# A two-layer hybrid decoder trunk: the first SwiGLU takes the stages of the inner ones, and the first norm's factors change place

## The chip, the core and the metric

The kernel runs on one core of a Trainium2 chip. The metric is device time in microseconds (us) of one execution, the median of the runs shown; lower is better. In the text the engines are TensorE (PE in the profile, its weight loads PEld), VectorE (DVE), ScalarE (ACT), GpSimd (POOL) and SyncE (SP). Each runs its own queue of instructions in order and waits on semaphores for the others. DMAs are issued from the queues of SP, ACT and POOL. L12 is line 12 of the kernel.

## What is computed

512 tokens of width 1024, two layers, each with a SwiGLU, a mixer (attention and short convolution) and a second SwiGLU, all float32 at the edges. The part that matters here:

```python
D_MODEL, SEQ, DEPTH, D_FF = 1024, 512, 2, 2816

def rms_norm(x, gain):
    inv = lax.rsqrt(jnp.mean(x * x, axis=-1, keepdims=True) + NORM_EPS)
    return x * inv * gain

def swiglu(h, w_gate, w_up, w_down):
    return (jax.nn.silu(h @ w_gate) * (h @ w_up)) @ w_down

for l in range(DEPTH):
    x = x + 0.5 * swiglu(rms_norm(x, ffn1_norm[l]), ffn1_wg[l], ffn1_wu[l], ffn1_wd[l])
    h = rms_norm(x, mix_norm[l])
    z = h @ w_in[l]                     # q, k, v and three convolution streams
    x = x + concat([attention(z), short_conv(z)]) @ w_out[l]
    x = x + 0.5 * swiglu(rms_norm(x, ffn2_norm[l]), ffn2_wg[l], ffn2_wu[l], ffn2_wd[l])
return rms_norm(x, final_norm)
```

## The kernel before

**Layout.** x is kept transposed, channels on partitions: eight tiles xs[c] of 128 channels x 512 tokens. At the start the token rows of x are loaded (xin), turned by TensorE (turn_x) and copied into xs (copy_x).

**Products in two parts.** Each float32 operand is split into a high part in a rounded format (a cast on ScalarE) and the rest (a subtraction on VectorE): `split`, L228. A product is three matmuls: high by high, high by low, low by high. Weight tiles are 128 x 1024 elements (512 KB), loaded into the tag "raw" (8 buffers) and split into "wh" and "wl" (3 buffers each). `take_split` hands out the next one and asks for the split two further on and for loads further ahead. A split marked "far" (`split_far`, L230) leaves VectorE out: ScalarE writes the high part and the negative, and a DMA on POOL's queue adds the raw tile to it.

**Blocks, pairs and shared down products.** The inner width 2816 is 11 blocks of 256. A "p" stage (`plain`) computes one block with the tile multiplied straight: four groups of 24 matmuls of 512 columns, two for the gate and two for up, then the split of the product. It uses the tile before the norm's factor, and multiplies by the factor `norm.inv` afterwards. A "w" stage (`winograd2`) computes two blocks with seven products in place of eight: weights of both are combined (s1, s2, s3, s4: sums by DMA in POOL's queue and by VectorE, L267 and L299), and the normed tile is combined into seven forms b11, b21, t2, t3, t1, t4, b22 of 1024 elements, each with a split of its own (`Seven.make`; the sums for t2, t3, t1 and t4 are additions on VectorE). It goes in seven steps in the order of CHAINS, two weight tiles each, 12 matmuls of 512 columns a tile, with tokens standing in the array (`stream`, L832). For this a norm first needs its factors, then eight scaled tiles hf (`Norm.scale`, L561). A "u" stage (`winograd`, L1013) is the same for one block, with 256 columns a matmul. A "d" stage is a straight down product of one block or two, whose eight results are added to xs (L1327). An "s" stage (`share`) is a down product of four blocks by seven products: either weights standing and 256 columns a matmul (`stand`, L817), added to xs directly, or tokens standing and 512 columns (`stream`), collected apart in rows of tokens (`Apart`) and turned back, by DMA in three quarters and by eight TensorE transposes in the last.

**Stages.** The first SwiGLU of layer 0 runs the list FIRST: two plain blocks, four pairs, a single block 10 by "u", and down products with weights standing. Layer 0's second SwiGLU and layer 1's first run INNER: one plain block, five pairs, shared down products with tokens standing, and a last straight down product of two blocks. The last SwiGLU has a list of its own.

**Order.** Most instructions are ordered by a planner at build time, in the program's order where they are ready. The opening (from `with tc.manual_schedule`, L721) is ordered by hand on TensorE, ScalarE and VectorE: spin, turn x, split the first three weight tiles in halves (`own`), form the split tile (`take`), squares of x for the norm (`squares`, four sets), and the products of groups 0 to 2 (`go`). The factors of the first norm (`first_parts`, two diagonal matrices, then two matmuls "ssq" and a copy into inv on ScalarE) are made behind it, within group 3. A warm-up at the start loads ScalarE's table for Silu. The mask for attention (`make_bias`, twelve small VectorE operations) is made behind the second down product.

Of the kernel before, what the change touches and what calls it, by code (L numbers as in the profile page):

```python
# [16 lines left out]
P = 128  # L17
D = 1024
# [59 lines left out]
def trunk_kernel(  # L78
# [157 lines left out]
    def need_split(g):  # L236
        while state["split"] <= min(g, len(order) - 1):
# [31 lines left out]
            else:  # L269

                need_raw(u + 4 + LOAD_AHEAD)
                a11, a12, s1, s3, a22 = (raw_of.get(u + i) for i in range(5))
                if what == "s2":
                    nc.vector.tensor_add(a11, a11, s1)
                if what == "s4":
                    nc.vector.tensor_add(a11, a11, a12)
                raw = {"a11": a11, "a12": a12, "s2": a11, "s3": s3, "s1": s1, "a22": a22, "s4": a11}[what]
                if what == FORMS[-1]:
                    for i in range(5):
                        del raw_of[u + i]  # L280
# [91 lines left out]
    def plan():  # L372
# [10 lines left out]
        def up(wg, wu, b):  # L383
            top, low = ((w, k, KC // 2, 2 * b * P, 2 * P) for w, k in ((wu, 0), (wu, KC // 2)))
            first = (wg, 0, KC // 2, 2 * b * P, 2 * P)
            u = add_unit(first)
            add_unit((wg, KC // 2, KC // 2, 2 * b * P, 2 * P))
            add_unit(top, low)
            add_unit(top, first)
            add_unit(low)  # L390
            order.extend((u, what) for what in FORMS)

# [9 lines left out]
        def ffn(wg, wu, wd, stages):  # L402
            for what, b in stages:
                how = "far" if b == (0,) and stages is not FIRST else None
                if what == "p":
                    plain(wg, wu, b)
                if what == "u":
                    up(wg, wu, b)
# [26 lines left out]
        for l in range(DEPTH):  # L435
            ffn(ffn1_wg[l], ffn1_wu[l], ffn1_wd[l], INNER if l else FIRST)
# [26 lines left out]
    class Norm:  # L463
        def __init__(self, i):
            self.i = i
            self.h = [None] * KC
            self.acc = None
            self.inv = None
            self.pairs = {}
            self.begun = set()  # L470
            self.order = range(KC)
# [85 lines left out]
        def scale(self, room):  # L557

            full = [g8(f"hf_{self.i}_{n}", F32, (P, KC // 2, S)) for n in range(2)]
            for c in range(KC):  # L560
                nc.vector.scalar_tensor_tensor(  # L561
                    full[c // 4][:, c % 4, :],
                    xs[c],
                    gain_of(self.i, c),
                    self.inv,
                    op0=ALU.mult,
                    op1=ALU.mult,
                )
            self.seven = Seven(full, room, f"{self.i}")
            self.make, self.forms = self.seven.make, self.seven.forms  # L570

    class Seven:
# [8 lines left out]
        def make(self, *names):  # L581
            for what in names:
                if what in self.forms:
# [3 lines left out]
                    full[j][:, :, t * H : (t + 1) * H] for j in range(2) for t in range(2)  # L587
# [39 lines left out]
    def room_stock(name):  # L627
        return [stock(f"sum{n}_{name}", shape=(P, KC // 2, H)) for n in range(2)]

# [30 lines left out]
    nc.scalar.activation(warm, warm, AF.Silu)  # L660
# [59 lines left out]

    with tc.manual_schedule(engines={pe, act, dve}):  # L721
# [19 lines left out]
        squares(0)  # L741
# [1057 lines left out]
```

## Time and profile before

| | us |
|---|---|
| median of 3 runs | 1640.02 |
| lowest and highest run | 1639.68, 1640.02 |
| profiled execution: span from first to last instruction | 1637.9 |
| TensorE busy in it | 1627.8 (99%) |
| VectorE busy | 1378.1 (84%) |
| ScalarE busy | 1141.7 (70%) |
| HBM read | 262.71 MB |

Of the profiled execution the span alone is listed; what lies before its first and behind its last instruction is not in it. In a row of the timeline the first number is the start in us from the span's start, the second the length, then engine, line, operation, output and inputs by their names in the program, shape, count, and in brackets how long the engine stood idle before and what ended that. "x2" after a shape means that two instructions of a kind follow each other without a pause. Matmuls are pipelined, and the length shown for one (390 ns for 512 columns) is longer than the step to the next.

### The profile page before, as it was taken

The page shows a single profiled execution, that of the slowest core. Times are in us where ns is not written, and L with a number is a line of the kernel's source. Part 1 is how long each engine was busy: PE and PEld are TensorE (multiplying, and loading weights), DVE is VectorE, ACT ScalarE, POOL GpSimd, SP SyncE. Part 2 cuts the span into 40 slices and gives each one's busy share as a digit, 9 for nine tenths or more (in the row PEclk, how much of TensorE's full clock was granted, in tenths as well). Part 3 has the DMA queues.
Part 4 walks back from the last instruction along what each step waited for, and adds up shares of the span by engine and source line. Part 5 has one row for each costly group of instructions (what it writes and reads, how often), then busy time and mean ns, then how long its engine had stood idle before and what let it go on. Part 6 is the DMA issues. An engine that isn't in the chain of part 4 may idle for free.

```text
span 1637.9 us, 21943 instructions
## 1 busy us (share of the span) xinstructions
PE 1627.8 (99%) x8012; PEld 1373.7 (84%) x8012; DVE 1378.1 (84%) x1812; ACT 1141.7 (70%) x1479; POOL 213.1 (13%) x188
## 2 busy tenths in 40 slices
PE   9999999999999999999999999999999999999998
PEld 7888889988898888888888888888888988888886
DVE  7987779987899977798998777989788998777997
ACT  6447786467767577777865777788586766777665
POOL 0011111100121011111011111110012111111121
PEclk9999999999999999999999999999999999999999
DMA  8378997742597698999866999998135967999992
GB/s 258 84 199 213 220 251 181 172 135 65 130 231 177 179 223 206 218 220 237 232 144 173 226 215 226 207 239 219 52 91 153 233 142 190 226 219 224 237 258 74
DMA packets 293984, 310.30 MB, mean 189 GB/s; under 512 B 110508, under 2 KB 179188, under 8 KB 293876
## 3 DMA queue, kind: packets, MB, share of 16 engines
q1 hardware_dynamic: 253284, 226.44, 48.1%
q0 software_dynamic: 39872, 81.80, 29.2%
q8 instruction: 63, 1.03, 0.3%
q10 hardware_dynamic: 720, 0.66, 0.1%
q14 instruction: 45, 0.37, 0.1%
HBM read 262.71 MB, written 2.10 MB: 162 GB/s over the span
## 4 chain that ended last, share of the span: by engine, by line
PE 90%; DVE 5%; ACT 3%; DMA 1%; issue 1%; SPq 0%; ACTq 0%; DVEq 0%
PE x L832 25%; PE y L832 13%; PE acc L326 7%; PE acc L327 7%; PE acc L329 7%; PE w L832 6%; PE x_s L832 5%; PE x_m L817 3%; PE y_s L832 3%; PE x_s L817 2%; PE w_s L832 2%; PE y_s L817 1%; PE y_m L817 1%; DVE wl L228 1%; PE acc L712 1%; PE x_e L832 1%
## 5 line engine op out<-in xcount | busy, mean ns | idle before, releaser
L228 ACT CAST wh<-raw 128x1024 fp32r<-128x1024 f32 (+1 forms) x491 | 511.1, 1045 | 346.0 <-PE x L832 91.4
L228 DVE TENSOR_TENSOR wl<-raw,wh 128x1024 fp32r<-128x1024 f32 (+1 forms) x491 | 598.1, 1226 | 175.7 <-ACT wh L228 174.3
L327 PE MATMUL acc<-xl,wh 128*128 128x512 f32 x424 | 165.9, 391 | 0.2 <-DVE xl L482 0.2
L326 PE MATMUL acc<-xh,wh 128*128 128x512 f32 x424 | 165.6, 392 | 0.0
L329 PE MATMUL acc<-xh,wl 128*128 128x512 f32 x416 | 162.3, 390 | 0.0
L223 POOL DMA_DIRECT2D raw<-in_ffn_wu_dram x39 | 48.8, 1252 | 392.9 <-DMA raw<-in_ffn_wu_dram 233.7
L327 PEld LDWEIGHTS acc<-xl,wh 128*128 128x128 f32 x424 | 79.7, 188 | 16.5 <-DVE xl L482 0.6
L326 PEld LDWEIGHTS acc<-xh,wh 128*128 128x128 f32 x424 | 79.8, 188 | 15.9
L329 PEld LDWEIGHTS acc<-xh,wl 128*128 128x128 f32 x416 | 78.2, 188 | 16.3
L223 POOL DMA_DIRECT2D raw<-in_ffn_wg_dram x39 | 48.2, 1259 | 231.5 <-DMA raw<-in_ffn_wu_dram 115.4
L223 POOL DMA_DIRECT2D raw<-in_ffn_wd_dram x34 | 41.0, 1209 | 244.6 <-DMA raw<-in_ffn_wd_dram 95.8
L267 DVE TENSOR_TENSOR raw<-raw,raw 128x1024 f32<-128x1024 f32 x56 | 68.1, 1222 | 2.3 <-DMA raw<-in_ffn_wu_dram 1.8
L1163 ACT COPY raw_a<-turned 128x1024 uint16<-128x1024 uint16 x48 | 63.1, 1356 | 0.0
L832 PE MATMUL w<-wh,fb21h 128*128 128x512 f32 x152 | 59.2, 390 | 0.0
L832 PE MATMUL x<-wh,ft2h 128*128 128x512 f32 x152 | 59.2, 390 | 0.0
L832 PE MATMUL y<-wh,ft3h 128*128 128x512 f32 x152 | 59.2, 390 | 0.0
L832 PE MATMUL x<-wh,ft1l 128*128 128x512 f32 x152 | 59.1, 389 | 0.0
L832 PE MATMUL x<-wl,ft1h 128*128 128x512 f32 x152 | 59.1, 389 | 0.0
L832 PE MATMUL w<-wl,fb21h 128*128 128x512 f32 x152 | 59.1, 389 | 0.0
L832 PE MATMUL x<-wl,ft2h 128*128 128x512 f32 x152 | 59.1, 389 | 0.0
L832 PE MATMUL w<-wh,fb21l 128*128 128x512 f32 x152 | 59.1, 389 | 0.0
L832 PE MATMUL x<-wh,ft2l 128*128 128x512 f32 x152 | 59.1, 389 | 0.0
(611 smaller groups left out, 4649.2 us busy)
## 6 DMA issues: line engine op xcount, KB each, us to landing
raw<-in_ffn_wu_dram SPq DMA_DIRECT2D x126, 512.0 KB, 5.3
raw<-in_ffn_wd_dram SPq DMA_DIRECT2D x105, 512.0 KB, 5.8
raw<-in_ffn_wg_dram SPq DMA_DIRECT2D x86, 512.0 KB, 5.3
raw<-in_ffn_wu_dram POOLq DMA_DIRECT2D x39, 512.0 KB, 8.9
raw<-in_ffn_wg_dram POOLq DMA_DIRECT2D x39, 512.0 KB, 6.1
raw<-in_w_in_dram SPq DMA_DIRECT2D x36, 512.0 KB, 4.1
raw<-in_ffn_wd_dram POOLq DMA_DIRECT2D x34, 512.0 KB, 9.5
raw<-raw POOLq DMA_DIRECT2D x21, 512.0 KB, 7.5
```

The lines of the kernel that those rows point to most:

```text
L223: nc.gpsimd.dma_start(out=r, in_=rows_of(*more), accum_op=ALU.add)
L228: return nc.scalar.copy(hi, raw), eng.tensor_sub(lo, raw, f32(hi))
L267: nc.vector.tensor_add(a11, a11, s1)
L326: nc.tensor.matmul(acc, hi[:, k, :], rhs[k][0], start=k == first, stop=False)
L327: nc.tensor.matmul(acc, hi[:, k, :], rhs[k][1], start=False, stop=False)
L329: nc.tensor.matmul(acc, lo[:, k, :], rhs[k][0], start=False, stop=k == last)
L712: nc.tensor.matmul(opening[n], (lo if part == "w" else hi)[:, k, :], xl if part == "x" else xh, start=n not in begun, stop=k == KC - 1 and ...
L817: nc.tensor.matmul(accs[c // 2][:, c % 2, :], w[:, k, cols], x_[:, 2 * h + k, :], start=start and c % 2 == 0 and h + k + i == 0, stop=h + ...
L832: nc.tensor.matmul(accs[u], x_[:, 2 * h + k, tok], w[:, k, :], start=start and h + k + i == 0, stop=h + k == 2 and i == 2, skip_group_chec ...
L1163: nc.scalar.copy(words(raws[self.b][:, c, :]), self.to[:, :, c, :])
```

## The change

The list FIRST, the stage "u" with its plan and `winograd`, and the special cases that went with them are gone. The first SwiGLU runs INNER: "p" 0, "d" (0,), five pairs 1, 3, 5, 7, 9, "s" 1, "s" 5, "d" (9, 10). In its first down product the weight splits stay on VectorE (near), while other INNER runs send them far. `Norm.scale` can do one half of hf at a time; the first SwiGLU does one half, the form b11, and then the other. The sums of its forms take a place among the tiles "g8" instead of two weight buffers. In the opening, squares 1 to 3 move ahead, `first_parts` and the factors go between the parts of group 2, with copies of x in another order, and ScalarE's warm-up loads the table for the reciprocal square root. The gates of groups 0 and 1 come ahead of group 3, and the mask's operations come ahead of pair 3.

```diff
-FIRST = (
-    ("p", 0), ("p", 1), ("d", (0,)), ("w", 2), ("d", (1,)), ("w", 4), ("w", 6), ("w", 8), ("u", 10),
-    ("s", 2), ("d", (10,)), ("s", 6),
-)
 INNER = (
     ("p", 0), ("d", (0,)), ("w", 1), ("w", 3), ("w", 5), ("w", 7), ("w", 9), ("s", 1), ("s", 5),
     ("d", (9, 10)),
...
-        def ffn(wg, wu, wd, stages):
+        def ffn(wg, wu, wd, stages, near=False):
             for what, b in stages:
-                how = "far" if b == (0,) and stages is not FIRST else None
+                how = "far" if b == (0,) and not near else None
...
-            ffn(ffn1_wg[l], ffn1_wu[l], ffn1_wd[l], INNER if l else FIRST)
+            ffn(ffn1_wg[l], ffn1_wu[l], ffn1_wd[l], INNER, l == 0)
...
             accs = list(accs) or [group(self.h, order=self.order)]
-            parts = self.parts()
+            parts = None if self.inv else self.parts()
             while len(accs) < n:
-                at, step = (1, 2) if self.i else (OPEN, 4)
-                due = len(accs) == at
+                due = parts and len(accs) == 1
                 accs.append(
-                    group(self.h, lambda k, hi, lo: due and k == step and self.factors(parts))
+                    group(self.h, lambda k, hi, lo: due and k == 2 and self.factors(parts))
                 )
...
-        def scale(self, room):
...
+        def scale(self, halves=(0, 1)):
+
+            for half in halves:
+                self.full.append(g8(f"hf_{self.i}_{half}", F32, (P, KC // 2, S)))
+                for c in range(4 * half, 4 * half + 4):
+                    nc.vector.scalar_tensor_tensor(
+                        self.full[half][:, c % 4, :],
+                        xs[c],
+                        gain_of(self.i, c),
+                        self.inv,
+                        op0=ALU.mult,
+                        op1=ALU.mult,
+                    )
...
-    nc.scalar.activation(warm, warm, AF.Silu)
+    nc.scalar.activation(warm, warm, AF.Abs_reciprocal_sqrt, bias=eps)
...
         squares(0)
+        squares(1)
         go(1, 0, 4, "hx")
         go(1, 0, 4, "w")
...
         own(0, 4, 8)
-        squares(1)
-        for c in range(3, 6):
+        squares(2)
+        for c in (6, 3):
             copy_x(c)
         go(0, 4, 8, "hwx")
         own(1, 4, 8)
+        squares(3)
         own(2, 4, 8)
-        for c in (6, 7):
+        copy_x(7)
+        go(1, 4, 8, "hx")
+        go(1, 4, 8, "w")
+        parts = first_parts()
+        for c in (4, 5):
             copy_x(c)
-        for n in (1, 2):
-            go(n, 4, 8, "hx")
-            go(n, 4, 8, "w")
+        go(2, 4, 8, "hx")
+        norm.factors(parts)
+        go(2, 4, 8, "w")
         for n in range(OPEN):
             del raw_of[n]
         state["split"] = state["group"] = OPEN
-        squares(2)
         need_split(OPEN)
-        squares(3)
...
-            if norm.inv is None:
-                accs = norm.groups(4, opening if first else [])
+            if norm.i:
+                accs = norm.groups(4)
                 gate(accs[0])
                 gate(accs[1])
-                norm.scale(room_stock if first else room_g8)
+                norm.scale()
                 up(0, accs[2])
-                if not first:
-                    norm.make("b11")
+                norm.make("b11")
                 up(1, accs[3])
             else:
...
+                gate(opening[0])
+                gate(opening[1])
+                accs = norm.groups(4, opening)
+                up(0, accs[2])
+                up(1, accs[3])
+                norm.scale((0,))
                 norm.make("b11")
...
+                norm.scale((1,))
...
-        apart = None if first else Apart(f"{norm.i}")
+        apart = Apart(f"{norm.i}")
...
             elif what == "w":
+                if late and b == 3:
+                    late()
...
-            for c, acc in down(rhs, b == (0,) and not first, final):
+            for c, acc in down(rhs, b == (0,), final):
                 if b == (0,):
-                    made = {0: "t3", 4: "t1"} if first else {0: "b21", 2: "t2", 5: "t3"}
+                    made = {0: "b21", 2: "t2", 5: "t3"}
...
-            if b == (1,) and late:
-                late()
...
-        ffn(norm, INNER if l else FIRST, into(n1), None if l else make_bias)
+        ffn(norm, INNER, into(n1), None if l else make_bias)
```

More of the change, by code (lines that the diff above doesn't have):

```diff
@@ L942, in ffn @@
         acts = {}
-        first = stages is FIRST
         def plain(b):
@@ L1292, in ffn @@
                     apart,
-                    behind=(0, 2, 3) if first else (),
                     still=kept,
                 )
-            elif what == "s" and i + 1 == len(stages):
-                share(then, 0.5, after.step, on=kept)
             elif what == "s":
```

167 lines of the change are left out of this document (31 added, 136 removed).

## The prediction

> **What bounds the kernel now.** I read the page first: its span, its engine line and the shares of the chain that ended last.
>
> ```profile
> span 1637.9 us, 21943 instructions
> PE 1627.8 (99%) x8012; PEld 1373.7 (84%) x8012; DVE 1378.1 (84%) x1812; ACT 1141.7 (70%) x1479; POOL 213.1 (13%) x188
> PE 90%; DVE 5%; ACT 3%; DMA 1%; issue 1%; SPq 0%; ACTq 0%; DVEq 0%
> ```
>
> TensorE is the bound: a matmul taken off it is worth its issue gap, as long as nothing else stops it. A mean busy time doesn't give that gap, as matmuls overlap, so I took it from stretches in which TensorE never stops. The next view cuts its time by stage. The columns are start and end, length, busy time, instructions, clock, DMA share and rate.
>
> ```profile
> 33.41:342.26 308.85, 308.47 (x1754) 1.00 0.78 189
> 845.92:1146.83 300.91, 300.78 (x1330) 1.00 0.90 214
> 115.15:229.39 114.24, 114.24 (x505) 1.00 0.90 214
> 301.95:342.26 40.31, 40.31 (x338) 1.00 0.70 180
> 342.26:500.37 158.11, 157.84 (x900) 1.00 0.53 134
> 1146.83:1305.59 158.76, 158.29 (x899) 1.00 0.50 129
> ```
>
> Row 1 is the first SwiGLU behind its first block, up to the first mixer. Row 2 is the same stretch of layer 1's first SwiGLU, which already runs the INNER stages: from its first down product to its mixer. Row 3 is three pairs, 504 matmuls of 512 columns: 114.24/504 = 226.7 ns each. Row 4 is a down product with weights standing, 336 matmuls of 256 columns: 120.0 ns each, so two of them cost 13.3 ns more than one of 512. (An edge adds one or two to a count.) Rows 5 and 6 are the two mixers.
>
> **The change, part by part.** *Stages.* Behind the first block FIRST issues 1008 matmuls of 512 columns and 840 of 256, less the 96 of block 0: plain block 96, downs 3 x 48, four pairs 4 x 168; block 10 has 168 and the two down products 336 each at 256 columns. INNER issues 1320 of 512 (down 48, five pairs and two down products 7 x 168, last down 96) and eight transposes. By the gaps that is 912 x 0.2267 + 840 x 0.120 = 307.5 us against 1320 x 0.2267 = 299.2 us and about 1 us of transposes. The measured rows 1 and 2 have the small stalls and the transposes in them, so I take their difference: 308.85 - 300.91 = **7.94 us saved**, if the first SwiGLU runs as smoothly as layer 1's.
>
> A rule speaks against this. The Trainium skill (TensorE: Matmul & The Clock Gate, Back-to-back issue gap) gives N/2.4 + 2.5 ns: 215.8 ns for 512 columns and 109.2 ns for 256, so that cutting a matmul in two costs next to nothing. By it the gain of the matmuls would be 3.6 us where the gaps above give 8.3, and the forecast 4.7 us higher, 1643.4. Rows 3 and 4 measure both gaps in this kernel, and they decide.
>
> *Into the mixer.* The new last stage hands over column by column, as layer 1's does. Rows 5 and 6 differ by 158.76 - 158.11 = 0.65 us; I take **+0.65**, with 0 as the other end.
>
> *The opening.* These are rows of the timeline in order of time; the squares that the factors need end with the row at 24.05.
>
> ```profile
> 17.83 0.65 ACT L690 ACTIVATE xsq<-xin 128x512 f32<-128x512 f32 x1
> 19.06 1.15 ACT L228 CAST wh<-raw 128x512 fp32r<-128x512 f32 x2
> 21.98 1.29 DVE L685 COPY x<-xt 128x512 f32<-128x512 f32 x2
> 24.05 0.19 ACT L690 ACTIVATION_READ_ACCUMULATOR xsq<-xin 128x1 f32 x1
> 25.19 1.28 ACT L772 ACT_TABLE_LOAD   x1
> 26.28 1.07 PE L712 MATMUL acc<-xh,wl 128*128 128x512 f32 x4
> 26.48 0.30 ACT L772 ACTIVATE r<-v,eps 128x4 f32<-128x4 f32 x1
> 26.69 1.03 ACT L228 CAST wh<-raw 128x1024 fp32r<-128x1024 f32 x1
> 27.19 0.39 PE L326 MATMUL acc<-xh,wh 128*128 128x512 f32 x1
> 28.37 0.69 DVE L781 TENSOR_TENSOR diag<-ident,yl 128x512 fp32r<-128x512 f32 x1
> 29.00 0.62 PE L547 MATMUL ssq<-diag,ones_r 128*128 128x512 f32 x2
> 29.66 0.59 ACT L550 COPY inv<-ssq 128x512 f32<-128x512 f32 x1 [1.94 <-PE ssq L547]
> 33.41 0.50 PE L326 MATMUL acc<-xh,wh 128*128 128x512 f32 x1
> ```
>
> The squares move ahead: a set of two (1.2 us, 17.83 to 19.06), one cast (0.6), and the last set, which so ends near 20.9; the table load at 25.19 falls away, since the warm-up now loads that set. With VectorE's copies in between, the chain (sum, root, three steps, two diagonals, 2.3 us from the root's end at 26.78 to 29.06) ends near 25.5. The two ssq products go in at 26.28, behind the third group's products of the upper rows, and cost no wait, with 0.8 us to spare. inv is then ready at 26.28 + (30.25 - 29.00) = 27.53 instead of 30.25. But the order written by hand puts the weight cast of group 3 behind the copy of inv on ScalarE: copy at 26.94, cast from 27.45 to 28.5 (1.03). TensorE is through with group 2 at 27.19 + 0.46 = 27.65 and waits 0.85 us; group 3's 24 matmuls end at 34.0, against 33.2 (33.41 with a small transpose that now fits in the wait). **+0.6**, with -0.2 (cast in time) and +1.2 as ends.
>
> *VectorE behind the factors.* This is the large term. A SwiGLU's pair 1 needs eight scaled tiles, seven forms with their sums, the down product's eight sums into x, and a split of each weight tile, all on VectorE. Layer 1 does this behind its own inv (ready at 834.40). The first row is VectorE's busy time by the view of windows, the others its timeline.
>
> ```profile
> 834.42:877.77 43.35, 42.46 (x49) 1.00 0.66 144
> 833.71 0.69 DVE L461 SCALAR_TENSOR_TENSOR inv<-mean,root 128x512 f32<-128x512 f32 x1
> 861.82 1.23 DVE L228 TENSOR_TENSOR ft1l<-hf,ft1h 128x1024 fp32r<-128x1024 f32 x1
> 862.96 2.36 DVE L267 TENSOR_TENSOR raw<-raw,raw 128x1024 f32<-128x1024 f32 x2
> 865.23 1.23 DVE L617 TENSOR_TENSOR sums<-sums,hf 128x1024 f32<-128x1024 f32 x1
> 866.36 2.37 DVE L228 TENSOR_TENSOR wl<-raw,wh 128x1024 fp32r<-128x1024 f32 x2
> 868.63 1.29 DVE L1074 TENSOR_TENSOR gate<-w,p 128x512 f32<-128x512 f32 x2
> 869.83 1.23 DVE L228 TENSOR_TENSOR ft4l<-sums,ft4h 128x1024 fp32r<-128x1024 f32 x1
> 870.96 1.23 DVE L228 TENSOR_TENSOR wl<-raw,wh 128x1024 fp32r<-128x1024 f32 x1
> 872.10 1.23 DVE L299 TENSOR_TENSOR raw<-raw,raw 128x1024 f32<-128x1024 f32 x1
> 874.37 1.24 DVE L299 TENSOR_TENSOR raw<-raw,raw 128x1024 f32<-128x1024 f32 x1
> 875.50 1.24 DVE L228 TENSOR_TENSOR fb22l<-hf,fb22h 128x1024 fp32r<-128x1024 f32 x1
> 876.63 2.37 DVE L228 TENSOR_TENSOR wl<-raw,wh 128x1024 fp32r<-128x1024 f32 x2
> 879.65 1.23 DVE L228 TENSOR_TENSOR wl<-raw,wh 128x1024 fp32r<-128x1024 f32 x1 [0.64 <-ACT wh L228]
> ```
>
> From inv on VectorE is busy 42.46 of 43.35 us, and its first real pause is at 879.65. Pair 1 begins there at 845.92 + 48 x 0.2267 = 856.8, 22.4 us behind inv. The split that ends the stretch (876.63, the first of two) is for step 4; TensorE needs it behind 98 matmuls of the pair, at 856.8 + 22.2 = 879.0, and has it at 877.8: 1.2 us to spare. In the changed kernel the pair would begin at 34.0 + 10.9 = 44.9, only 17.4 us behind inv, as one group and not three still run behind it. And three more splits fall into the stretch: group 3's, and the two of the down product, which layer 1 sends through ScalarE and a DMA ("far") and the changed plan does not; 3 x 1.14 (the step in the x2 rows) = 3.4. VectorE can begin once its last copies of x are made, about 26.75 (chain to 25.5, two copies of 0.6, as at 21.98): 26.75 + 42.46 + 3.4 = 72.6. TensorE wants that split at 44.9 + 22.2 = 67.1: 5.5 us late. I take **+5.4**, as the order may put a product of the other accumulator ahead. It would show as several waits of 1 to 3 us in steps 0 to 4 of pair 1, not one. Both ends: ft4 with its sum, fb22 and the two raw sums (5 x 1.14 = 5.7) aren't due by step 4; served after the splits they'd leave **0**. The rows show them served first, in the program's order. At the other end, all lateness is carried: 22.4 - 17.4 + 3.4 = 8.4, less 0.6 to spare at step 2 (split of 866.36 done at 867.5, needed at 856.8 + 22.2 - 10.9 = 868.1): **7.8**.
>
> *Costed at nothing.* The mask's operations now come ahead of pair 3:
>
> ```profile
> 115.96 2.09 DVE L806 SCALAR_TENSOR_TENSOR bias<-dist,mask 128x256 bf16<-128x256 f32 x6
> 22.09 2.70 SPq L211 DMA_DIRECT2D raw<-in_ffn_wg_dram  x2
> DMA to landing us min/median/max: 4.4/7.6/9.0
> ```
>
> They are twelve of about 0.35 us, 4.2 us as an estimate from the first row; VectorE's pauses in the last three steps of pair 1 take them, and without that cover they cost up to 4.2. Loads: units 10 and 11 are issued from 22.09 on in the queue of weights; in the new plan these are the third weights of pair 1, needed near 50, so SyncE's queue is ahead. The first weights of the pair go the far way: ScalarE is free for them when group 3 ends, near 36.3; with a median of 7.6 us from issue to landing (last row) they are there at 43.9, with 1.4 us in hand for the third matmul; at 9.0 there is none left, 0 to 0.5.
>
> **Sum.** All trace times are of the profiled execution, whose span is 1637.9; the median of 1640.02 lies 2.1 above it, and I leave that as it is. 1640.02 - 7.94 + 0.65 + 0.6 + 5.4 = **1638.7 us**.
>
> **Rivals.** *VectorE keeps up.* The order puts due splits first, and the wait is 0: 1633.3. For it: only 5.7 us need to change places. Against it: the rows above, where fb22l (due at step 6) stands ahead of step 4's split.
>
> *The factors come no sooner.* If the copies of x or the squares hold the chain back, the two products stand at the head of TensorE's queue at 26.28 and everything waits behind them, up to 2.7 us (to 29.00 as now): 1641.4. For it: the chain crosses between ScalarE and VectorE several times in an order fixed by hand. Against it: the 0.8 us in hand.
>
> *VectorE doesn't clear its queue within pair 1* (the slower side). The lateness is the whole 7.8, its pauses in steps 4 to 6 are used up by it, and the mask's 4.2 us stand ahead of pair 3's splits and are paid too: 1640.02 - 7.94 + 0.65 + 0.6 + 7.8 + 4.2 = 1645.3. It decides once VectorE has under about 3 us of pauses between step 4 and the end of pair 1. For it: no pause of a microsecond before 879.65 in layer 1 either. Against it: behind that row TensorE's 5.44 us a step meet two splits and two small operations, some 3.7 us.
>
> **Chances.** Forecast 0.50, its own range 1636.3 to 1640.8 by waits of 3 to 7.5 us; keeps up 0.28; factors late 0.08; not cleared 0.14. A measurement of this kernel tells about 0.2%, 3.3 us, from no change: faster is below 1636.7, slower above 1643.3. Faster: 0.28 and 0.06 of the forecast, 0.34. Within: 0.44 and 0.08, 0.52. Slower 0.14. The range runs from 1632.8 (no wait, and the smaller ends of the small terms) to 1641.7 (7.8, and the small terms as taken, with factors a little late) and leaves out the last rival.
>
> **What would show it.** Right: ssq products at about 26.3 and inv near 27.5; a wait of 0.8 us before the first L326 matmul; VectorE without a pause from there to step 4 of pair 1; 4 to 7 us of TensorE's waits on splits or x sums between 45 and 80; then 252 us from the end of pair 1 to the mixer, as in layer 1; a first mixer of 158.8. Wrong: pair 1 in 38.1 us without waits, or a fall of the granted clock in those waits, or waits behind pair 1.

## The result, and the profile after

The changed kernel takes 1644.73 us (median of 11 runs, 1642.98 to 1648.77); the kernel before, run beside it, 1639.95 (11 runs, 1638.87 to 1641.80). The ratio is 1.0029, with a 95% interval of 1.002 to 1.0037: 4.8 us slower. The forecast was 1638.7 us, 1.2 us faster, with a range up to 1641.7.

The profiled execution took 1644.6 us and has a span of 1642.8, 4.9 above the span of before. First the page of the changed kernel: its span, its engine line and the shares of the chain that ended last.

```profile
span 1642.8 us, 21157 instructions
PE 1623.4 (99%) x7588; PEld 1349.7 (82%) x7588; DVE 1375.2 (84%) x1787; ACT 1169.0 (71%) x1498; POOL 216.5 (13%) x191
PE 80%; DVE 9%; ACT 5%; DMA 3%; issue 2%; POOL 0%; SPq 0%; ACTq 0%; DVEq 0%; POOLq 0%
```

TensorE's busy time fell by 4.4 us (1627.8 to 1623.4), as a change with fewer matmuls should make it, and yet the span grew. In the chain that ended last TensorE's share fell from 90 to 80%, VectorE's rose from 5 to 9 and that of DMA from 1 to 3. That points at VectorE; what each stage lost is read from the next view.

The view of windows of the changed kernel, by stage (start and end, length, busy time of TensorE with its instructions, then the other engines, granted clock, DMA share and rate):

```profile
34.47:344.72 310.25, 303.01 (x1330) 247.72 (x1328) 261.25 (x286) 222.76 (x252) 36.11 (x32) 1.00 0.86 206
45.37:89.98 44.61, 39.67 (x170) 31.00 (x168) 41.90 (x44) 24.20 (x29) 2.39 (x2) 1.00 0.51 138
89.98:130.88 40.90, 38.73 (x170) 31.38 (x168) 31.14 (x41) 27.22 (x32) 5.62 (x6) 1.00 0.87 218
45.37:245.12 199.75, 192.64 (x842) 157.01 (x840) 163.85 (x176) 136.88 (x158) 22.03 (x19) 1.00 0.82 200
861.93:1052.33 190.40, 190.40 (x841) 157.71 (x840) 152.57 (x155) 135.01 (x156) 22.96 (x19) 1.00 0.88 213
344.72:505.22 160.50, 158.96 (x900) 137.75 (x898) 136.38 (x280) 110.47 (x193) 22.67 (x18) 1.00 0.51 128
1151.93:1310.50 158.57, 158.22 (x900) 138.00 (x899) 135.64 (x278) 110.73 (x193) 22.67 (x18) 1.00 0.51 128
```

Row 1 is the first SwiGLU behind its plain block, which was 308.85 us long in the kernel before. Rows 2 and 3 are pair 1 and pair 3, rows 4 and 5 the five pairs here and in layer 1, where TensorE is busy for the whole stretch: 190.40, or 38.08 a pair. So pair 1 lost 44.61 - 38.08 = 6.53 us and pair 3 lost 40.90 - 38.08 = 2.82; the other three lost nothing (199.75 - 190.40 - 6.53 - 2.82 = 0). Rows 6 and 7 are the two mixers. Set against the kernel before, term by term:

| term | forecast | this execution |
|---|---|---|
| stages, without waits | -7.94 | 310.25 - 6.53 - 2.82 - 308.85 = -7.95 |
| opening | +0.6 | 34.47 - 33.41 = +1.06 |
| VectorE late in pair 1 | +5.4 | +6.53 |
| mask, ahead of pair 3 | 0 | +2.82 |
| first mixer | +0.65 | 160.50 - 158.11 = +2.39 |
| sum | -1.3 | +4.85 |

What TensorE waited for, by the view of waits of the changed kernel between 45 and 104 us (waiting engine and line, releaser, us in total, times, longest):

```profile
PE x L806 <- DVE wl L224: 2.1, 2, 1.1
PE w L806 <- DVE x L1228: 2.1, 1, 2.1
PE w L806 <- DVE wl L224: 1.5, 2, 1.1
PE y L806 <- ACT wh L224: 1.4, 2, 0.9
```

None is for a transfer. Five of these waits lie in pair 1; in pair 3 there are two, of 1.1 us each, on splits. Three of the four releasers are VectorE's: splits of weights, and a sum into x that frees the PSUM bank (the place of a result until VectorE has taken it) of the first w product. The fourth is ScalarE's. The first of its two casts (0.9 us) stood in ScalarE's queue behind a form that waited for VectorE:

```profile
58.31 1.05 ACT L224 CAST ft1h<-hf 128x1024 fp32r<-128x1024 f32 x1 [5.36 <-DVE hf L590]
```

The second (0.5 us) stood behind a copy of a product of TensorE's own, so it is not VectorE's. This view counts from the modelled end of the matmul before, so its 7.1 us are less than the 9.3 of the windows.

VectorE in the same stretch, from its timeline:

```profile
27.91 1.29 DVE L923 TENSOR_TENSOR gate<-acc,inv 128x512 f32<-128x512 f32 x2 [0.94 <-ACT inv L524]
...
53.00 1.88 DVE L1228 SCALAR_TENSOR_TENSOR x<-acc,x 128x512 f32<-128x512 f32 x3
...
73.03 3.48 DVE L224 TENSOR_TENSOR wl<-raw,wh 128x1024 fp32r<-128x1024 f32 x3
77.94 1.22 DVE L224 TENSOR_TENSOR wl<-raw,wh 128x1024 fp32r<-128x1024 f32 x1 [1.43 <-ACT wh L224]
...
95.67 0.29 DVE L773 CAST dist<-dist_i 128x256 f32<-128x256 int32 x1 [1.65 <-POOL dist_i L771]
...
100.03 2.77 DVE L780 SCALAR_TENSOR_TENSOR bias<-dist,mask 128x256 bf16<-128x256 f32 x8
102.71 2.35 DVE L224 TENSOR_TENSOR wl<-raw,wh 128x1024 fp32r<-128x1024 f32 x2
```

It starts on inv at 27.91, and its first pause of a microsecond or more ends at 77.94. The last three sums into x, which free a PSUM bank, run until 54.9, nine microseconds after the down product that made them (it ended at 45.37). Up to 95.67 it stands 1.65 us with nothing to do, waiting for the iota of the mask (the row of distances that the mask is made from), with pair 3's splits behind it. GpSimd's timeline says why the iota is late:

```profile
92.85 2.42 POOL L219 DMA_DIRECT2D raw<-in_ffn_wg_dram  x2 [10.79 <-DMA raw<-in_ffn_wu_dram]
94.77 0.87 POOL L771 IOTA dist_i<- 128x256 int32 x1
```

It stands in GpSimd's queue behind two accumulating loads, and those waited for a plain load to land.

### The profile page after: what moved, and what is told of

Read it like the earlier page. It is cut to its first block, busy times and chain, and to the rows that moved or that the text cites. A ratio compares the mean times of both kernels' runs of the same rounds, so it can differ in the third digit from the quotient of the medians.

```text
span 1642.8 us, 21157 instructions
## 1 busy us (share of the span) xinstructions
PE 1623.4 (99%) x7588; PEld 1349.7 (82%) x7588; DVE 1375.2 (84%) x1787; ACT 1169.0 (71%) x1498; POOL 216.5 (13%) x191
## 4 chain that ended last, share of the span: by engine, by line
PE 80%; DVE 9%; ACT 5%; DMA 3%; issue 2%; POOL 0%; SPq 0%; ACTq 0%; DVEq 0%; POOLq 0%
PE x L806 25%; PE y L806 13%; PE x_s L806 7%; PE w L806 6%; PE acc L311 4%; PE acc L310 4%; PE acc L313 4%; PE y_s L806 4%; DVE wl L224 3%; PE w_s L806 2%; PE x_m L791 2%; ACT wh L224 1%; PE y_m L791 1%; PE acc L684 1%; PE x_e L806 1%
## 5 line engine op out<-in xcount | busy, mean ns | idle before, releaser
L311 PE MATMUL acc<-xl,wh 128*128 128x512 f32 x392 | 153.4, 391 | 0.3 <-DVE xl L457 0.3
L310 PE MATMUL acc<-xh,wh 128*128 128x512 f32 x392 | 153.1, 392 | 0.5 <-ACT wh L224 0.5
L313 PE MATMUL acc<-xh,wl 128*128 128x512 f32 x384 | 149.8, 390 | 0.0
L311 PEld LDWEIGHTS acc<-xl,wh 128*128 128x128 f32 x392 | 73.7, 188 | 15.5 <-DVE xl L457 1.0
L310 PEld LDWEIGHTS acc<-xh,wh 128*128 128x128 f32 x392 | 73.8, 188 | 15.2 <-ACT wh L224 0.6
L313 PEld LDWEIGHTS acc<-xh,wl 128*128 128x128 f32 x384 | 72.2, 188 | 14.9
L806 PE MATMUL w<-wh,fb21h 128*128 128x512 f32 x160 | 62.5, 391 | 2.1 <-DVE x L1228 2.1
L806 PE MATMUL x<-wl,fb11h 128*128 128x512 f32 x160 | 62.2, 390 | 1.0 <-DVE wl L224 1.0
L806 PE MATMUL y<-wh,ft4h 128*128 128x512 f32 x160 | 62.3, 390 | 0.5 <-ACT wh L224 0.5
```

Of the source, the lines that this page charges most:

```text
L310: nc.tensor.matmul(acc, hi[:, k, :], rhs[k][0], start=k == first, stop=False)
L311: nc.tensor.matmul(acc, hi[:, k, :], rhs[k][1], start=False, stop=False)
L313: nc.tensor.matmul(acc, lo[:, k, :], rhs[k][0], start=False, stop=k == last)
L806: nc.tensor.matmul(accs[u], x_[:, 2 * h + k, tok], w[:, k, :], start=start and h + k + i == 0, stop=h + k == 2 and i == 2, skip_group_chec ...
```

## The experiments

The ratio of each kernel below to the kernel before stands beside its median, with its 95% interval; the kernel before took 1639.64 to 1639.95 us beside them. As the medians carry a microsecond or two of chance, the stage lengths of the profiled executions are given with them: from the first matmul of the first down product to the end of the pairs (210.65 us in the changed kernel), or, where the opening differs, from the first weight product (237.80).

```profile
34.47:245.12 210.65, 203.54 (x890) 166.01 (x888) 174.75 (x191) 141.82 (x164) 25.31 (x22) 1.00 0.83 201
7.32:245.12 237.80, 230.14 (x1014) 186.72 (x1013) 196.04 (x228) 161.91 (x204) 27.92 (x24) 1.00 0.84 211
```

**The mask ahead of pair 7.**

```diff
-                if late and b == 3:
+                if late and b == 7:
                     late()
```

> The mask is made ahead of pair 7 instead of pair 3; nothing else differs from the changed kernel. Theory (VectorE's queue: the wait for the iota and twelve mask operations stand ahead of pair 3's splits, behind a pair that left VectorE no lead): the two waits in pair 3 (1.29 and 1.21 us) go, pair 7 shows at most 0.5 us, time 2 to 2.5 us below the changed kernel's 1644.7, so about 1642.5. Rival 1 (the sums by DMA of pair 3's weights land late whatever VectorE does): the waits of pair 3 stay, time unchanged within 0.5 us. Rival 2 (the mask costs wherever it stands): the 2.5 us reappear in pair 7.

Measured: 1641.19 us, ratio 1.0003 (0.9994 to 1.0012), 3.5 below the changed kernel. The window view of this kernel:

```profile
35.65:243.44 207.79, 202.85 (x890) 166.14 (x888) 174.68 (x191) 141.48 (x164) 25.32 (x22) 1.00 0.84 203
```

207.79 against 210.65: 2.86 us gone, the 2.82 that pair 3 had lost, and no wait came up in pair 7. Both rivals fall. The median gained more than the 2 to 2.5 us expected and somewhat more than the stage; its interval holds the stage's gain too.

**The iota alone made early.** GpSimd makes it behind the opening, into a tile that stays; VectorE's twelve operations remain ahead of pair 3.

```diff
+    di = const.tile([P, 2 * P], I32, name="dist_i")
+    nc.gpsimd.iota(di, pattern=[[-1, 2 * P]], base=P, channel_multiplier=1)
+
     def make_bias():
-        di = g2("dist_i", I32, (P, 2 * P))
-        nc.gpsimd.iota(di, pattern=[[-1, 2 * P]], base=P, channel_multiplier=1)
```

> GpSimd makes the iota of the mask behind the opening, into a tile of its own; the twelve VectorE operations of the mask stay ahead of pair 3 as in the changed kernel. Theory 1 (the mask's price is VectorE's idle 1.65 us, as the iota stands in GpSimd's queue behind two accumulating loads that wait for their tiles): pair 3's waits fall from 2.50 to at most 0.9 us, time 1.5 to 2.5 below 1644.7. Theory 2 (the price is the operations' own 4.3 us): the waits stay at 2 us or more. Both in halves: 1 to 1.4 us left.

Measured: 1642.63 us, ratio 1.0020 (1.0012 to 1.0029), 2.1 below the changed kernel.

```profile
34.08:242.72 208.64, 203.13 (x890) 166.10 (x889) 174.69 (x191) 141.77 (x164) 24.92 (x21) 1.00 0.83 205
```

Of 2.86 us, 210.65 - 208.64 = 2.01 went with the iota, as the first theory had it. So the mask's price was for the most part the wait in GpSimd's queue; some 0.85 us were left for its own operations.

**Forms one step ahead.** The first SwiGLU makes t2, t3, t1, t4 and b22 shortly before pair 1 uses them.

```diff
                 norm.make(operand)
+                if not norm.i and 2 <= step < 6:
+                    norm.make(CHAINS[step + 1][1])
...
                     stream(accs[acc], wh, wl, xh, xl, h, start)
+                    if not norm.i and step == h == 0:
+                        norm.make("t2")
...
-                if step < 3:
+                if norm.i and step < 3:
                     norm.make(CHAINS[step + 4][1])
...
-                    made = {0: "b21", 2: "t2", 5: "t3"}
+                    made = {0: "b21"} if not norm.i else {0: "b21", 2: "t2", 5: "t3"}
```

> In the first SwiGLU the forms t2, t3, t1, t4 and b22 of the token operand are made about one step before pair 1 uses them, no longer up to four steps ahead; the count of instructions is the same. Theory (VectorE's queue is served in its order, and work that is not yet due stands ahead of splits that are): the waits in pair 1 fall from 6.5 us to 2.5 to 3.5 us, the one for the PSUM bank of the first w product (2.27) goes, since the eight sums into x end some 3.5 us sooner, and a new one of 1 to 2 us for ft2 takes its place; time 3 to 4 us below 1644.7, about 1641. Rival 1 (VectorE's total work up to step 4 sets the lateness, whatever its order): waits stay at 6 us or more. Rival 2 (weights' transfers or ScalarE's casts are late): the waits on wh or on raw weights stay as they are.

Measured: 1639.35 us, ratio 0.9992 (0.9984 to 1.0001), 5.4 below the changed kernel. Windows and waits of this kernel (the second window is pair 1; the waits are those between 26 and 104 us, and the one ahead of group 3, 0.5, is left out):

```profile
34.12:240.38 206.26, 203.01 (x890) 166.19 (x888) 174.68 (x191) 141.89 (x164) 25.29 (x22) 1.00 0.84 205
45.01:87.66 42.65, 39.50 (x170) 31.14 (x168) 41.88 (x44) 24.27 (x29) 2.39 (x2) 1.00 0.55 155
```

```profile
PE x L806 <- DVE ft1l L224: 1.3, 1, 1.3
PE x L806 <- ACT wh L224: 0.8, 1, 0.8
...
PE x L806 <- DVE ft2l L224: 0.4, 1, 0.4
PE x L806 <- DVE wl L224: 0.4, 1, 0.4
PE x L806 <- ACT ft1h L224: 0.3, 1, 0.3
```

4.39 us gone from the stages. VectorE's busy time is the same to 0.1 us (174.68 and 174.75), so this is not less work. In pair 1 itself the gain was 44.61 - 42.65 = 1.96 us, less than expected: 4.57 us stayed, between the theory's 2.5 to 3.5 and the first rival's 6. The wait for the PSUM bank is no longer there, and new ones are there on ft2 and ft1, the latter not expected. The other 2.4 us came from pair 3, which took 38.48 us (126.14 - 87.66) and lost only 0.40, although the mask stood where it was. In this execution VectorE waited 0.76 us for the iota and not 1.65, so two things may have helped there: the shorter wait, and a VectorE that came less late out of pair 1. No run parts them.

**VectorE's work lengthened.** The four scaled tiles of the second half are written twice.

```diff
-                for c in range(4 * half, 4 * half + 4):
+                for c in (*range(4 * half, 4 * half + 4),) * (1 if self.i or not half else 2):
```

> The four scaled tiles of the second half are written twice (four VectorE operations of 128x512 more, about 2.7 us), between the first block and pair 1; the numbers computed are the same. Theory (VectorE's queue paces pair 1, one for one): pair 1's waits grow from 6.5 to about 9.2 us, time 2.2 to 3 us above 1644.7, about 1647.3, and no other engine's first pause moves. Rival (transfers, ScalarE or PSUM pace it and VectorE only looks full): less than 1 us more.

Measured: 1646.15 us, ratio 1.0035 (1.0024 to 1.0047), 1.4 above the changed kernel, less than expected. Given the intervals the medians alone can't tell this from no change or from the 2.2 to 3 expected; the traces say more.

```profile
34.12:247.57 213.45, 205.87 (x889) 167.67 (x888) 177.48 (x195) 142.00 (x164) 25.28 (x22) 0.98 0.81 198
53.91:60.73 6.82, 5.65 (x14) 3.78 (x14) 6.82 (x9) 1.18 (x2) 0.00 (x0) 0.50 0.01 2
```

```profile
80.63 1.23 DVE L224 TENSOR_TENSOR wl<-raw,wh 128x1024 fp32r<-128x1024 f32 x1 [1.46 <-ACT wh L224]
```

In the profiled execution the stages took 213.45 - 210.65 = 2.80 us more, for 177.48 - 174.75 = 2.73 more of VectorE: one for one. The end of VectorE's first pause of a microsecond moved as far, from 77.94 to 80.63. Hardly any of it shows as waits: TensorE's idle time in the stages grew by 0.5 us only (213.45 - 205.87 against 210.65 - 203.54). A wait of 2.8 us, from 50 to 53, was followed by 6.8 us at half the granted clock (second row), and slow matmuls took the place of the waits that would have come. The delay followed VectorE's queue, whether TensorE waited or crept. The whole span grew by 0.6 us only, as the first mixer took 158.95 us here and 160.50 in the changed kernel; that term varies by itself, as told below.

**The factors made late again.** The new stages, but with the factors where the kernel before makes them; group 3 comes ahead of the gates again for this.

```diff
-        parts = first_parts()
...
-        norm.factors(parts)
         go(2, 4, 8, "w")
...
-                due = parts and len(accs) == 1
+                at, step = (1, 2) if self.i else (OPEN, 4)
+                due = parts and len(accs) == at
```

> The new stages with the factors of the first norm made where the kernel before makes them, behind the third group's upper rows in the planner's part, so that inv comes some 2 us later; the rest as in the changed kernel. Theory (VectorE, from inv on, paces pair 1): the wait of 0.66 us ahead of group 3 goes, pair 1 begins 0.7 us sooner, and its waits grow by 2.5 to 3 us, time 1.5 to 2.5 us above 1644.7, about 1646.7. Rival (the opening costs what it costs, and pair 1's waits come from elsewhere): time 0.6 us below 1644.7.

Measured: 1645.17 us, ratio 1.0026 (1.0016 to 1.0036), 0.4 above the changed kernel: by the medians it can't be told from it.

```profile
6.79:246.04 239.25, 231.11 (x1012) 187.81 (x1012) 196.50 (x228) 162.16 (x204) 27.95 (x24) 0.99 0.84 211
35.53:38.94 3.41, 2.85 (x7) 2.28 (x8) 2.88 (x5) 1.02 (x2) 1.71 (x3) 0.50 1.09 241
```

```profile
PE acc L329 <- ACT a L224: 2.7, 1, 2.7
```

The stages took 239.25 - 237.80 = 1.45 us more, and the main wait moved: the first down product now waits 2.7 us for the block's output, and at its end the clock goes to half for 3.41 us. That is the direction of the theory and less than its size. This profiled execution was the slowest of the kernel's nine (1648.38 us), so the sooner factors are worth something like 0.4 us by the medians and 1.5 by this trace, and the two don't settle it.

**The opening alone.** The kernel before, with its own stages, and only the new opening and the table loaded at the warm-up.

> The kernel before with only the second half of the change: its own first stages, but the opening that makes the first norm's factors sooner, and the table loaded at the warm-up. Theory: the kernel before has no waits behind the opening that a sooner inv could take away, and group 3 now waits 0.66 us for its cast behind inv; time 0.2 to 0.8 us above the kernel before, about 1640.2. Rival 1 (the opening itself is what costs): 2 us or more above. Rival 2 (a sooner inv helps any stages): below the kernel before.

Measured: 1640.47 us, ratio 1.0004 (0.9995 to 1.0013). As expected, 0.7 above the kernel before and hardly to be told from it. The waits of this kernel between 4 and 60 us:

```profile
PE xt L678 <- DMA xin<-in_x_dram: 1.6, 1, 1.6
PE acc L326 <- ACT wh L228: 0.5, 1, 0.5
```

The second is the wait that the forecast named. The first is a load of the input that lands sooner or later from run to run; it is met again below. So most of the loss of 4.8 us is the stages' and not the opening's; with the factors late the new stages lost as much.

**Group 3's cast ahead of inv.**

```diff
         go(2, 4, 8, "hx")
-        norm.factors(parts)
-        go(2, 4, 8, "w")
         for n in range(OPEN):
             del raw_of[n]
         state["split"] = state["group"] = OPEN
         need_split(OPEN)
+        norm.factors(parts)
+        go(2, 4, 8, "w")
```

> In the opening group 3's weight cast on ScalarE and its split on VectorE stand ahead of the copy of inv and of the gates, no longer behind them; nothing else differs from the changed kernel. Theory (VectorE's queue paces everything up to step 5 of pair 1): the wait of 0.66 us ahead of group 3 goes, the split fills the 0.94 us that VectorE waited for inv, pair 1 begins 0.7 us sooner and its waits stay at 6 to 6.5 us, time 0.6 to 1.0 us below 1644.7. Rival (pair 1 is paced by something that does not begin sooner, transfers or inv itself): the 0.66 us come back as waits in pair 1 and the time stays within 0.2 us.

Measured: 1641.96 us, ratio 1.0017 (1.0008 to 1.0025), 2.8 below the changed kernel; 236.16 us of stages in the trace, 1.64 less. More than expected: the planner drew a second split ahead of inv too, so VectorE was at work from 26.54 on without the two pauses (0.94 and 0.47 us) that it had around inv. The pauses gone, 1.41 us, and the time gained, 1.64, are again about one for one. The wait ahead of group 3 went, and one of 1.5 us ahead of the first down product came.

**Three edits together**: forms one step ahead, mask ahead of pair 7, and pair 1's two sums a12 + a11 made by an accumulating DMA.

```diff
-                if what == "s3" and how == "share":
+                if what == "s3" and how in ("share", "sum"):
                     nc.gpsimd.dma_start(out=a12, in_=a11, accum_op=ALU.add)
...
-                        lambda what, h: "far" if (b, what, h) == (1, "a11", 0) else None,
+                        lambda what, h: "far" if (b, what, h) == (1, "a11", 0) else "sum" if near and b == 1 else None,
```

> Three edits together: forms made one step ahead, mask ahead of pair 7, and in pair 1 the two sums a12 + a11 made by an accumulating DMA instead of VectorE (two operations of 1.135 us less). Theory (VectorE's queue): of the 3.98 us of waits that the forms' edit alone left in pair 1, the two on ft1 (0.43 and 1.46) go, some 2.1 us on ft2 and its weights stay, pair 3 shows none; the five pairs take 192.5 to 193.3 us, and the time is about 1637.3, 2.6 below the kernel before. Rival (the DMA sum lands late): a wait of 1 us or more on wh at step 5 of pair 1.

Measured: 1636.49 us, ratio 0.9983 (0.9974 to 0.9991); the five pairs took 193.34 us. In pair 1 only the waits on ft2 and its weights are left, and the DMA's sums caused none; pair 7, with the mask ahead of it, took 38.64 us and lost 0.56. As expected, within a microsecond, and faster than the kernel before by 0.2%.

**These and the cast ahead of inv.**

> The three edits of the run before and the cast of group 3 ahead of inv. Theory: no wait ahead of group 3, the waits on ft2 in pair 1 no longer than there; 0.6 to 1.0 us below the run before, about 1636.5. Rival (the order of the opening only moves the wait): the same time within 0.3 us.

Measured: 1634.93 us, ratio 0.9976 (0.9968 to 0.9985); 230.05 us of stages against 237.80. A further 1.6 by the medians, more than the 0.6 to 1.0 expected; the pairs took 191.04, and a wait of 1.5 us for the first block's output stood ahead of the first down product.

**The gates ahead of the next casts.** As the last, but the casts and splits of the first down product's weights are kept behind the gates.

```diff
-                nc.scalar.activation(t, t, AF.Silu)
+                state["silu"] = nc.scalar.activation(t, t, AF.Silu).ins
...
-                accs = norm.groups(4, opening)
+                with tc.issue_after(state["silu"]):
+                    accs = norm.groups(4, opening)
```

> As the run with the four edits (forms one step ahead, mask at pair 7, two sums by DMA, group 3's cast ahead of inv), but the weights of the first down product are cast and split behind the gates of the first block, as in the changed kernel, and no longer ahead of inv. Theory (VectorE's queue up to step 2 of pair 1 holds a fixed sum of work, and its order only says where TensorE waits for it): the 1.62 us ahead of the first down product go, 1 to 1.5 us come back as waits on ft2 and its weights; the time is that of the run before within 0.7 us, about 1634.6. Rival (the order is worth its whole wait): 1.6 us less, about 1633.3.

Measured: 1635.04 us, ratio 0.9969 (0.9957 to 0.9980).

```profile
7.50:237.51 230.01, 228.72 (x1011) 187.23 (x1012) 193.48 (x226) 162.12 (x204) 29.63 (x26) 1.00 0.89 222
```

230.01 against 230.05. The wait ahead of the down product is gone, and as much came back on ft2 and its weights. So it looks as if a fixed sum of VectorE's work stood ahead of step 2 of pair 1, and only less of it would help from here; the next run tries that.

**Less of it: GpSimd makes two of the sums.**

```diff
+                    if not norm.i and c == 1:
+                        low, high = norm.full
+                        norm.seven.differences(nc.gpsimd, low[:, :, :H], low[:, :, H:], high[:, :, H:])
```

> As the run with the gates ahead, and GpSimd makes the two differences behind t2 and t3 (128x1024 each) instead of VectorE, while the first down product runs. Theory (VectorE's queue, 2.27 us shorter ahead of step 2): the 1 to 1.5 us of waits on ft2 and its weights fall to at most 0.3, time 0.8 to 1.5 us below that run, about 1633.4. GpSimd's rows of 128x512 took 1.41 to 1.59 us, so two of 128x1024 end some 6 us after the scaled tiles at 43, near 50, in time for step 2 at 56. Rival 1 (GpSimd is later than that): a wait for ft2 of 1 us or more. Rival 2 (GpSimd and VectorE slow each other down): VectorE's 1.135 us a step grow while GpSimd works, and the gain is lost.

Measured: 1635.54 us, ratio 0.9974 (0.9965 to 0.9983); 230.45 us of stages: nothing gained. GpSimd was in time (its second sum ended at 47.79), so the first rival falls. GpSimd's and VectorE's timelines of this kernel:

```profile
42.05 2.40 POOL L558 TENSOR_TENSOR sums<-hf,hf 128x1024 f32<-128x1024 f32 x1 [0.88 <-DVE hf L536]
44.53 3.26 POOL L559 TENSOR_TENSOR sums<-sums,hf 128x1024 f32<-128x1024 f32 x1
```

```profile
43.09 2.45 DVE L224 TENSOR_TENSOR fb21l<-hf,fb21h 128x1024 fp32r<-128x1024 f32 x1
45.46 1.28 DVE L1240 SCALAR_TENSOR_TENSOR x<-acc,x 128x512 f32<-128x512 f32 x2
46.66 2.22 DVE L224 TENSOR_TENSOR wl<-raw,wh 128x1024 fp32r<-128x1024 f32 x1
```

Both splits of VectorE that fall into GpSimd's work take 2.45 and 2.22 us instead of 1.22. Each ends 1.1 us after GpSimd's operation does (44.45 and 47.79), as if it had stood still until then, while the sums into x, whose first input lies in PSUM, are not lengthened. VectorE paid 1.23 + 1.00 us for the 2.27 that it was relieved of. The second rival was right.

## Why the prediction was wrong, by its steps

**What bounds the kernel, and the stages: right.** Without waits the new stages save 7.95 us where 7.94 were forecast. The rule on issue gaps that spoke against this would have made it some 4.7 us less, and did not hold here.

**VectorE behind the factors: the mechanism right, the size 1.1 us short.** 6.53 us were lost in pair 1 where +5.4 was taken, in five waits of up to 2.1 us; all but one of 0.5 us go back to VectorE's splits, forms and sums into x, as forecast. That it is VectorE's queue, about one for one, is shown by lengthening it (2.73 us more, 2.80 us later) and by filling its pauses around inv (1.41 us of them gone, 1.64 sooner). That its order matters too is shown by reordering it (1.96 us less in pair 1 with the same work). The sum was made at one place, the split for step 4, and left out that the sums into x also hold a PSUM bank: two microseconds were lost on that at step 1. The lower end, 0 for a better order, was not reached by the order that was tried: with the forms one step ahead 4.57 us stayed in pair 1. The pairs came to 191.04 with less work on VectorE and a fuller use of its pauses around inv besides, and then 1.5 us stood ahead of the first down product.

**The mask, "costed at nothing": the step that failed.** It cost 2.82 us, the largest of the misses (first mixer 1.74, VectorE 1.13, opening 0.46). The forecast said that VectorE's pauses in the last three steps of pair 1 take its operations. The first such pause ended at 77.94, VectorE's pauses in the whole of pair 1 made 44.61 - 41.90 = 2.71 us, the operations were issued in pair 3, and their own time was the smaller part of the price. What was not looked at is the queue that the iota is moved past: GpSimd's, where it stands behind two accumulating loads. VectorE then waits for it with the splits of pair 3 behind. The iota made early took 2.01 of the 2.86 us away, the mask ahead of pair 7 all of it. The price hung on pair 1's lateness and on the iota's: with the forms one step ahead and the mask where it was, pair 3 lost 0.40. The forecast bounded this at "up to 4.2" and did not carry that bound into its range, which ended at 1641.7. The range was also off at its lower end: with the smaller ends as given (no wait, mixer 0, opening -0.2) the sum is 1640.02 - 7.94 - 0.2 = 1631.9, not 1632.8.

**The opening: right in kind.** TensorE's and ScalarE's timelines of the changed kernel, and TensorE's waits from 4 to 45 us:

```profile
26.63 0.62 PE L521 MATMUL ssq<-diag,ones_r 128*128 128x512 f32 x2
28.87 0.50 PE L310 MATMUL acc<-xh,wh 128*128 128x512 f32 x1 [0.49 <-ACT wh L224]
```

```profile
27.29 0.59 ACT L524 COPY inv<-ssq 128x512 f32<-128x512 f32 x1 [3.79 <-PE ssq L521]
27.77 1.05 ACT L224 CAST wh<-raw 128x1024 fp32r<-128x1024 f32 x1
```

```profile
PE xt L650 <- DMA xin<-in_x_dram: 1.0, 1, 1.0
PE acc L310 <- ACT wh L224: 0.5, 1, 0.5
```

The cast stands behind the copy of inv, and TensorE waits for it, 0.5 us where 0.85 was reckoned; the opening alone cost 0.7. The rest of the 1.06 is a load of the input, which TensorE waited 1.0 us for in this execution and not in that of before. Both kernels issue the loads up to there in the same order and within 0.1 us at the same times. But of the twelve profiled executions with the new opening ten had such a wait (0.3 to 1.6 us), and of the old opening there is one, without it. Whether the new opening brings it on is open.

**Into the mixer: mis-sized.** 2.39 us were lost where +0.65 was taken. In the eleven profiled executions with the new stages the first mixer took 158.5 to 160.5 us, so the term lies between 0.4 and 2.4, and this execution had the largest. The rows of ScalarE's timeline of the changed kernel, for the copies that wait for tiles turned by DMA, in layer 0 and in layer 1:

```profile
323.52 2.56 ACT L893 COPY back<-turned 128x1024 uint16<-128x1024 uint16 x2 [2.60 <-DMA turned<-halves]
...
1128.55 2.58 ACT L893 COPY back<-turned 128x1024 uint16<-128x1024 uint16 x2 [0.41 <-DMA turned<-halves]
```

The first begins 21.2 us ahead of its mixer, the second 23.4. VectorE came into the first mixer 1.0 us later for it, and two waits there, for xl and for pl, go back to VectorE. The three executions in which this copy began latest (20.4 to 21.3 us ahead of the mixer) had the three longest first mixers, 160.1 to 160.5; among the other eight (22.3 to 23.9 us ahead, 158.5 to 159.5) the two don't go together. That is a comparison of traces; no run was made to move the turns, so it is argued and not shown.

**The rivals.** "VectorE doesn't clear its queue within pair 1" came nearest, with 1645.3, by the right two causes, though with both sizes too high (7.8 and 4.2 for 6.53 and 2.82) and without the mixer's 1.74 more, so that its number came so near is in part luck. It was given 0.14. Its condition, under about 3 us of pauses from step 4 on, was met, with 2.71 in all of pair 1; the forecast had put 5.44 us a step against 3.7 of work there and taken the rest for free. "VectorE keeps up", 1633.3, is nearly where the best kernels arrived, which also took two sums off VectorE: 1634.9 and 1635.0, with some 2 us still lost in the pairs and ahead of the first down product.

**What would show it.** ssq at 26.63 and inv at 27.29 + 0.59 = 27.88 came nearly as forecast (26.3 and 27.5); pair 1's loss was 6.5 us, for 4 to 7. Of the signs named for being wrong, waits behind pair 1 were seen: from the end of pair 1 to the mixer it took 344.72 - 89.98 = 254.7 us, not 252.

## What to carry to other kernels

When work is moved to another place in a program, follow each of its instructions into the queue that it will stand in, also the small one on an engine that is nearly idle: its price is what stands ahead of it there, and what stands behind the engine that waits for it. When a stage is made shorter for the engine that bounds it, add up what the second engine has to do before each due time, not over the stage; here 9.3 us of waits ate a saving of 7.9 at a mean load of 84%. And order that engine's queue by due time before taking work off it: the order alone gave back 2.0 us in the pair that it was changed for, and 2.4 more behind it, where the iota also came sooner.

## What the hardware showed that was not expected

**The clock falls after waits of about 3 us and less.** Waits of up to 2.1 us left the granted clock at 1.00 in the changed kernel. After a wait of 2.7 us (factors late) it was at half for 3.41 us, after one of 2.8 (scaled tiles twice) for 6.82. In the run with four edits a late transfer in a later, unchanged stage made TensorE wait 3.1 us, and the clock was at half for 6.82 us:

```profile
PE y_s L806 <- ACT wh L224: 3.1, 1, 3.1
```

```profile
749.16:755.98 6.82, 6.20 (x14) 4.42 (x15) 6.26 (x7) 6.52 (x7) 1.21 (x1) 0.50 1.27 291
```

That stage took 83.46 us there, and 76.9 to 77.0 in the kernel before, the changed kernel and the run with three edits, so the wait was about doubled. (This execution took 1640.69 us, 5.8 above its kernel's median.) The length of one wait does not decide it by itself: with the factors late the clock fell once more, in layer 1's mixer, after two waits of 0.9 and 1.1 us with one matmul between them:

```profile
1158.52:1161.93 3.41, 3.31 (x8) 2.49 (x9) 2.61 (x5) 1.53 (x3) 0.00 (x0) 0.50 0.52 154
```

The Trainium skill (TensorE: Matmul & The Clock Gate, Part 1: The HAM clock gate) has the clock at half after an idle window of about 3.4 us. The two rates agree, and the stretches at half, 3.41 and 6.82 us, are once and twice that figure; the waits that were enough here were shorter.

**VectorE and GpSimd stop each other.** The rows of the GpSimd run show splits held until GpSimd's operation ended. The Trainium skill (SBUF — State Buffer, SBUF: two separate sides) says that a GpSimd operation, and a VectorE operation with two inputs in SBUF, take one port pair as a lock for the whole instruction. The trace agrees: the splits have two such inputs and doubled, the sums into x have one in PSUM and did not. GpSimd's second sum also took 3.26 us where its first took 2.40, as if it in turn had stood still while VectorE's split ran.
